# Measured spacings in the planner's prices of TensorE's matmuls and of VectorE's scalings and maxima

## The chip, the cores and the metric

The kernel runs on one core of one Trainium2 chip. The metric is the device time in microseconds of one execution, the median of several; lower is better.

## The reference

Two layers of a hybrid decoder on 528 tokens (16 learned meta tokens and 512 of input) of 1024 channels, in float32. Cut to what matters:

```python
for l in range(DEPTH):                       # DEPTH = 2
    xn = rms_norm(h, norm1_g[l])
    z, xbc, dt_raw, q, k, v, gate_logits = split(xn @ w_in[l])
    y_ssd = ssd_mixer(z, xbc, dt_raw, ...)   # width-4 conv, silu, chunked Mamba-2 scan, gated norm
    y_attn = sliding_window_attention(q, k, v, ...)  # 16 query heads, 4 kv heads, window 128, sinks
    g_ssd, g_attn = split(sigmoid(gate_logits + b_gate[l]))
    merged = g_ssd * (y_ssd @ w_ssd_down[l]) + g_attn * (y_attn @ w_attn_down[l])
    h = h + merged @ w_o[l]
    hn = rms_norm(h, norm2_g[l])
    h = h + square(relu(hn @ w_mlp_up[l])) @ w_mlp_down[l]
return h[:, 16:]
```

## The kernel before

Activations lie transposed: 128 channels on the partitions, 528 tokens along the row. A weight is read in tiles of 1024 input channels by 128 output channels (`wraw`, 512 KB). Products that need near-float32 precision are made of three fp32r products: ScalarE rounds a weight tile to its high half `whi`, POOL or VectorE subtracts to get the low half `wlo` (`weights`, `sub_any`), activations are split in the same way, and `dense` adds hi x hi, hi x lo and lo x hi over the eight blocks of input channels into one PSUM bank. Layer 0 runs its products on two spans of 264 tokens (266 for what the convolution reads); layer 1, whose meta tokens are needed only in part, mostly on one span of 512.

A layer goes through stages. At its start come the norm, v and dt, then k and q with rotary embedding. In the mixer the tiles of xs, B, C, z and the gates are streamed as dense products, and between these matmuls the small work of attention (`attention`) and of the SSD scan (`chunk`, `tail`) is threaded. Then come the two down projections, the output projection, and the MLP in four quarters, dense products almost alone.

Attention works in 36 blocks (five query blocks in layer 0 and four in layer 1, for each of 4 kv heads). A block computes scores in two pairs (`score`); VectorE adds the mask and takes the row maximum in one instruction (`top`, a `tensor_tensor_reduce`, seen in the trace as `CUSTOM_DVE_ANT_0`); ScalarE takes the exponential; VectorE scales four rows by the reciprocal of the sum (`tensor_scalar` on `at`, SBUF to SBUF, with a scalar per row). Then one to three pieces each go through transposes on TensorE, a copy to `ar` on ScalarE, a subtraction into `ar` on VectorE, and the product with v. An SSD chunk (80 of them, 72 of which need an output and 64 a state) has transposes, a state product, and an output of four products on 64 partitions each (`ps<-gm,xdt`).

The order of all of this is not written by hand. While the program is built, a planner (`Flow`) keeps a clock for each engine (`F.t`), adds to it the price of each instruction, and pins every instruction behind the one before it on its engine. A piece of small work is a `Task`, a generator; `dense` calls `tick` after every second matmul, and `tick` lets a task take its next step when its ready time is not later than TensorE's clock:

```python
if (calm or q is not self.queues["attn"]) and t.at(self) <= now:
    self.step(t, q)
```

`now` is `F.t["pe"]`. The ready time is the end of the step's last instruction plus `LATP` = 100 ns where TensorE is next. Where one engine reads what another wrote, `there` adds a hop (`HOP`): 198 ns from TensorE to ScalarE, 235 from VectorE to TensorE, 130 where none is listed. `busy` and `calm` hold steps back while VectorE's or ScalarE's clock is over 3500 ns ahead of TensorE's. `shares` and `turn` delay a VectorE instruction past a POOL instruction where both use the shared port: those of VectorE with two tensor operands in SBUF, or with one operand alone. A scaling by a per-row scalar counts as neither. `tt_any` chooses POOL or VectorE by which clock would end first; for weights VectorE is handed a penalty of 1200 ns. The SP queue's DMAs are pinned in the planner's order as well.

The steps of the change touch `Engine.cost` (the prices of VectorE, ScalarE and POOL) and `mm` (the prices of matmuls). In the trace all VectorE, ScalarE and POOL instructions have line L348, all matmuls L431, and transposes L434.

Of the kernel before, what the change touches and what calls it, by code (L numbers as in the profile page):

```python
# [14 lines left out]
PSUM = bass.MemoryType.PSUM  # L15
# [108 lines left out]
class Flow:  # L124
# [85 lines left out]
    def run(self, e, cost, outs, ins, inst):  # L210
        start = max(self.t[e], self.there(e, outs, ins))
        if self.shares(e, outs, ins):
            start = self.turn(e, start)
            held = self.port[e]
            held.append((start, start + cost))
            del held[:-16]
        self.t[e] = end = start + cost
        self.last = cost
        self.note(e, outs, ins, end)
        self.pin(e, inst)  # L220
# [86 lines left out]
class Engine:  # L307
# [12 lines left out]
    def cost(self, name, n, k, aps):  # L320
        scalars = sum(isinstance(k.get(x), bass.AP) for x in ("scalar", "scale", "bias", "mul"))
        if self._k == "v":
            if name == "reciprocal":
                return 6.4 * n + 60.0
            if name == "tensor_tensor_reduce":
                return n / 0.96 + 165.0
            return n / 0.96 + 62.0 + (58.0 if scalars else 0.0)
        if self._k == "s":
            psum = any(x.space == PSUM for x in aps)
            return n / 1.2 + (48.0 if psum else 86.0) + 93.0 * scalars + (95.0 if "accum_out" in k else 0.0)  # L330
        if k.get("op") == ALU.pow:
            return 190.0 * n + 120.0
        if name == "memset":
            return 40.0
        return n * (2.09 if name == "tensor_tensor" else 3.8) + 125.0
# [19 lines left out]
def hybrid_trunk_kernel(ctx: ExitStack, tc: tile.TileContext, h0, params, consts, rope, wdt, w, out,  # L355
# [69 lines left out]
    def mm(o, lhsT, rhs, start=True, stop=True):  # L425
        n = Engine.size(rhs)
        if rhs.dtype == F32R and n >= 256:
            cost = n / 2.4
        else:
            cost = max(n, 128) * 4 / 2.4 * (0.66 if o.shape[0] == 64 else 1.0)  # L430
        F.run("pe", cost, [o], [lhsT, rhs], PE.matmul(out=o, lhsT=lhsT, rhs=rhs, start=start, stop=stop))  # L431

    def transpose(o, in_, k=P):
# [89 lines left out]
    def dense(spans, tile_, act, evac, after=None, hold=False, by_row=None, late=None, more=(), keep=False):  # L523
# [15 lines left out]
        def product(p, ps, a, b, i):  # L539
            x, k = steps[i]  # L540
            last = p == len(parts) - 1
            if late and last and k >= KD - 2:
                late.pop()()
            whi, wlo = wt[parts[p][0]].slot.parts
            act = parts[p][1]
            mm(ps.t[:, :b - a], (wlo if x == 2 else whi)[:, k, :], (act.lo if x == 1 else act.hi)(k)[:, a:b],
               start=(p == 0 and i == 0), stop=(last and i == len(steps) - 1))
            if i % 2:
                F.tick()
                if held and all(t.done for t in first):  # L550
                    leave()
# [40 lines left out]
    def rms_tok(sq, inv_n, cs, tag, rows=(), bank="ps"):  # L592


        yield {bank: 1, "after": rows, "data": lambda: [x[:, CHUNKS[cs[0]][0]:sum(CHUNKS[cs[-1]])] for x in sq()]}
        ps = Slot("ps")
        for c in cs:
            t0 = CHUNKS[c][0]
            x = sq()
            for i in range(len(x)):  # L600
                mm(ps.t[:, c:c + 1], x[i][:, t0:t0 + P], C("ones"), start=i == 0, stop=i == len(x) - 1)
        yield
        r = sm.tile([P, 5], F32, name=tag, tag=tag)
        x = r[:, cs[0]:cs[-1] + 1]
        V.tensor_scalar(out=x, in0=ps.t[:, cs[0]:cs[-1] + 1], scalar1=inv_n, scalar2=EPS, op0=ALU.mult, op1=ALU.add)
        ps.free()
        G.tensor_tensor(out=x, in0=x, in1=C("mhalf")[:, cs[0]:cs[-1] + 1], op=ALU.pow)
        return r

    def bcast_tok(r, cs_, bank="ps"):  # L610

        for cs in ((0, 1, 2), (3, 4)):
            cs = [c for c in cs if c in cs_]
            if not cs:
                continue
            yield {bank: 1}
            ps = Slot("ps")
            lo, end = CHUNKS[cs[0]][0], sum(CHUNKS[cs[-1]])
            for c in cs:
                t0, n = CHUNKS[c]  # L620
                mm(ps.t[:, t0 - lo:t0 - lo + n], r[:n, c:c + 1].broadcast_to([n, P]), C("ident", n)[:, :n])
            yield ps, ps.t[:, 0:end - lo], lo, end
# [73 lines left out]
    for l in range(depth):  # L696
# [154 lines left out]
        for c in range(5):  # L851
# [4 lines left out]
            x = ps.t[:, 256:256 + NH]  # L856
# [867 lines left out]
```

## Time and profile before

| | us |
|---|---|
| median of 3 runs | 2446.96 (2444.26 to 2449.26) |
| profiled execution, its own time | 2436.77 |
| its span, first to last instruction | 2435.1 |
| busy: TensorE, VectorE, POOL, ScalarE | 2363.5, 1337.1, 1097.8, 1025.4 |

Busy time is the union of an engine's instructions. A matmul's duration in the trace (285 ns for 264 columns) overlaps that of the next one; the spacing from start to start is what it takes of TensorE. A float32 product has two matmul records, an fp32r product one.

### The profile page before, as it was taken

Reading aid. Unit: us, or ns where it says so; the run is one execution under the profiler, and the core shown is the slowest. Engines: PE = TensorE matmul, PEld = TensorE weight load, DVE = VectorE, ACT = ScalarE, POOL = GpSimd, SP = SyncE. Lnnn points to the kernel's source line nnn. Section 1 sums busy time; section 2 is a strip of 40 time slices with the busy share of each in tenths; the row PEclk is TensorE's granted clock in tenths of the full one; section 3 lists DMA queues with packets and bytes.
Section 4 is the critical chain, followed back from the end, with each engine's and each line's share of the span. In section 5 each row is a group of like instructions: output and inputs, shape, how many; then the busy total and the mean of one; then the engine's idle time right before and its main releaser. Section 6 shows DMA issues by size and latency. Waiting matters only on the chain.

```text
span 2435.1 us, 40407 instructions
## 1 busy us (share of the span) xinstructions
PE 2363.5 (97%) x16038; PEld 2143.3 (88%) x16038; DVE 1337.1 (55%) x2509; ACT 1025.4 (42%) x1999; POOL 1097.8 (45%) x651
## 2 busy tenths in 40 slices
PE   6999999999999999999999899999999999999999
PEld 6889899999999999999997788888988788888887
DVE  5787788787522444233246868787875135433221
ACT  4365566564432233222244456556554223333231
POOL 3534434465444334343434454445555543444443
PEclk9999999999999999999999999999999999999999
DMA  4323333343443322222232233324434533222222
GB/s 138 91 75 106 83 102 93 90 116 101 118 177 113 141 79 87 96 87 96 94 136 82 69 100 105 106 73 121 118 93 133 177 121 135 89 95 95 95 95 104
DMA packets 133578, 257.33 MB, mean 106 GB/s; under 512 B 16470, under 2 KB 66318, under 8 KB 133390
## 3 DMA queue, kind: packets, MB, share of 16 engines
q1 hardware_dynamic: 133390, 254.75, 33.4%
q8 instruction: 127, 2.08, 0.3%
q14 instruction: 61, 0.50, 0.1%
HBM read 232.03 MB, written 17.33 MB: 102 GB/s over the span
## 4 chain that ended last, share of the span: by engine, by line
PE 80%; DVE 12%; issue 3%; ACT 2%; POOL 2%; DMA 1%; SPq 0%; DVEq 0%; POOLq 0%; ACTq 0%
PE ps L431 78%; PE ps L434 2%; DVE xb L348 2%; DVE at L348 1%; DVE raw L348 1%; DVE xh L348 1%; DVE rqs L348 1%; DVE scr L348 1%; DVE gm L348 1%; POOL wlo L348 1%; DVE ar L348 1%; DVE mx L348 1%; DMA gm<-ac_dram 0%; DVE qa L348 0%; ACT at L348 0%
## 5 line engine op out<-in xcount | busy, mean ns | idle before, releaser
L348 POOL TENSOR_TENSOR wlo<-wraw,whi 128x1024 fp32r<-128x1024 f32 x328 | 797.5, 2431 | 982.7 <-ACT whi L348 930.4
L348 ACT CAST whi<-wraw 128x1024 fp32r<-128x1024 f32 x340 | 355.5, 1046 | 707.5 <-PE ps L431 421.4
L431 PE MATMUL ps<-hnh,whi 128*128 128x266 f32 (+2 forms) x2048 | 401.2, 312 | 5.3 <-DVE vm L348 4.6
L431 PE MATMUL ps<-hnl,whi 128*128 128x266 f32 (+2 forms) x2048 | 399.3, 311 | 0.0
L431 PE MATMUL ps<-hnh,wlo 128*128 128x266 f32 (+2 forms) x2048 | 391.8, 308 | 0.0
L431 PEld LDWEIGHTS ps<-hnh,whi 128*128 128x128 f32 x2048 | 307.2, 192 | 20.6 <-issue 6.8
L431 PEld LDWEIGHTS ps<-hnl,whi 128*128 128x128 f32 x2048 | 307.7, 192 | 15.1 <-issue 1.3
L431 PEld LDWEIGHTS ps<-hnh,wlo 128*128 128x128 f32 x2048 | 304.0, 190 | 15.2 <-issue 2.3
L348 DVE SCALAR_TENSOR_TENSOR h<-ps,h 128x264 f32<-128x264 f32 (+1 forms) x120 | 62.1, 517 | 308.8 <-PE ps L431 308.8
L348 DVE TENSOR_TENSOR hidl<-s,hidh 128x528 fp32r<-128x528 f32 (+1 forms) x64 | 116.9, 1827 | 88.1 <-ACT s L348 88.1
L431 PE MATMUL ps<-hgl,whi 128*128 128x264 f32 (+1 forms) x768 | 153.7, 322 | 1.3 <-DVE hgl L348 1.3
L431 PE MATMUL ps<-hgh,wlo 128*128 128x264 f32 (+1 forms) x768 | 153.4, 321 | 0.0
L431 PE MATMUL ps<-hgh,whi 128*128 128x264 f32 (+1 forms) x768 | 152.8, 321 | 0.0
L431 PE MATMUL ps<-hidl,whi 128*128 128x264 f32 (+1 forms) x768 | 152.6, 321 | 0.0
L431 PE MATMUL ps<-hidh,whi 128*128 128x264 f32 (+1 forms) x768 | 152.5, 320 | 0.0
L431 PE MATMUL ps<-hidh,wlo 128*128 128x264 f32 (+1 forms) x768 | 152.5, 320 | 0.0
L431 PE MATMUL ps<-y,whi 128*128 128x264 f32 (+1 forms) x768 | 137.0, 320 | 0.0
L431 PEld LDWEIGHTS ps<-hgl,whi 128*128 128x128 f32 x768 | 119.0, 188 | 12.4 <-DVE hgl L348 1.6
L431 PEld LDWEIGHTS ps<-hgh,wlo 128*128 128x128 f32 x768 | 119.5, 189 | 11.0
L431 PEld LDWEIGHTS ps<-hidl,whi 128*128 128x128 f32 x768 | 118.9, 188 | 11.0
L431 PEld LDWEIGHTS ps<-hidh,wlo 128*128 128x128 f32 x768 | 118.8, 188 | 11.0
L431 PEld LDWEIGHTS ps<-hidh,whi 128*128 128x128 f32 x768 | 118.7, 188 | 11.1
(218 smaller groups left out, 3947.5 us busy)
## 6 DMA issues: line engine op xcount, KB each, us to landing
wraw<-w_dram SPq DMA_DIRECT2D x344, 512.0 KB
gm<-ac_dram SPq DMA_DIRECT2D x64, 256.0 KB
et<-ac_dram SPq DMA_DIRECT2D x128, 64.0 KB
t<-au SPq DMA_DIRECT2D x48, 66.0 KB
h<-h_dram SPq DMA_DIRECT2D x8, 264.0 KB
at<-rope_dram SPq DMA_DIRECT2D x4, 528.0 KB
y_dram<-xb SPq DMA_DIRECT2D x4, 528.0 KB
yr<-y_dram SPq DMA_DIRECT2D x8, 264.0 KB
```

The costliest lines, as they stand in the source:

```text
L348: inst = fn(*a, **k)
L431: F.run("pe", cost, [o], [lhsT, rhs], PE.matmul(out=o, lhsT=lhsT, rhs=rhs, start=start, stop=stop))
L434: F.run("pe", 108.0 if in_.shape[1] > 64 else 60.0, [o], [in_], PE.transpose(out=o, in_=in_, identity=C("ident", k)[:, :k]))
```

## The change

Four prices of the planner are replaced. No instruction is added to the program or removed from it; the order in which the planner lays out the instructions, and its choices between POOL and VectorE, follow from the prices.

```diff
             if name == "tensor_tensor_reduce":
-                return n / 0.96 + 165.0
+                return n / 0.96 + 190.0
+            if name == "tensor_scalar" and not any(x.space == PSUM for x in aps):
+                return n / 1.92 + 62.0 + (58.0 if scalars else 0.0)
             return n / 0.96 + 62.0 + (58.0 if scalars else 0.0)
...
         if rhs.dtype == F32R and n >= 256:
-            cost = n / 2.4
+            cost = n / 2.25 + 4.0
         else:
-            cost = max(n, 128) * 4 / 2.4 * (0.66 if o.shape[0] == 64 else 1.0)
+            cost = max(n, 128) * 4 / 2.28 * (0.9 if o.shape[0] == 64 else 1.0)
```

## Rows read from the trace of the kernel before

**Rows 1.** The page's first part: busy us (share of span) and instructions.

```profile
PE 2363.5 (97%) x16038; PEld 2143.3 (88%) x16038; DVE 1337.1 (55%) x2509; ACT 1025.4 (42%) x1999; POOL 1097.8 (45%) x651
```

**Rows 2.** Busy time by stretch: us, engines with instruction counts, clock, DMA share, GB/s.

```profile
0.00:150.00 150.00, 124.81 (x933) 119.99 (x934) 96.37 (x209) 65.65 (x147) 67.76 (x49) 0.98 0.32 104
150.00:650.00 500.00, 486.71 (x3870) 454.72 (x3870) 393.60 (x881) 288.03 (x697) 239.57 (x173) 0.99 0.36 100
650.00:1270.00 620.00, 617.15 (x5051) 615.87 (x5051) 211.54 (x287) 184.17 (x247) 254.65 (x115) 1.00 0.32 112
1270.00:1400.00 130.00, 113.30 (x696) 98.19 (x696) 97.03 (x208) 57.59 (x114) 57.09 (x37) 0.95 0.23 71
1400.00:1850.00 450.00, 441.04 (x2952) 383.19 (x2951) 351.78 (x743) 258.24 (x579) 223.15 (x162) 0.99 0.38 104
1850.00:2435.00 585.00, 580.47 (x2547) 471.34 (x2545) 186.79 (x186) 171.75 (x218) 255.54 (x117) 1.00 0.33 113
```

**Rows 3.** TensorE's waits over the span: us in total, times, longest us.

```profile
PE ps L431 <- DVE acc L348: 13.9, 1, 13.9
PE ps L431 <- DVE mx L348: 6.5, 1, 6.5
...
PE ps L431 <- DVE adt L348: 3.8, 2, 3.1
...
PE ps L434 <- DVE at L348: 2.1, 2, 1.2
```

**Rows 4.** TensorE's waits from 150 to 650 us, first and last kind.

```profile
PE ps L431 <- DVE ar L348: 9.0, 8, 2.3
...
PE ps L431 <- POOL q L348: 0.5, 1, 0.5
```

**Rows 5.** TensorE's waits from 1400 to 1850 us, first and last kind.

```profile
PE ps L431 <- DVE ar L348: 5.5, 5, 1.9
...
PE ps L431 <- DVE zs L348: 0.2, 1, 0.2
```

**Rows 6.** Two dense stretches of 50 us, columns as in rows 2.

```profile
1000.00:1050.00 50.00, 50.00 (x414) 50.00 (x413) 14.66 (x21) 12.73 (x16) 21.36 (x9) 1.00 0.25 85
2150.00:2200.00 50.00, 50.00 (x218) 40.67 (x217) 13.25 (x13) 13.14 (x16) 21.70 (x10) 1.00 0.28 95
```

**Rows 7.** Tile ar: durations in ns min/median/max, first and last start, forms.

```profile
L348 DVE TENSOR_TENSOR ar<-ps,ar x92: 205/680/694, 124.8 to 1664.7; 128x512 fp32r<-128x512 f32 x56, 32x512 fp32r<-32x512 f32 x32, 16x64 fp32r<-16x64 f32 x4
```

**Rows 8.** Groups by form on VectorE: count, busy us, mean ns, idle before.

```profile
L348 DVE TENSOR_SCALAR at<-at,su 128x272 f32<-128x272 f32 x96 | 37.0, 448 | 0.9
...
L348 DVE TENSOR_SCALAR at<-at,su 128x144 f32<-128x144 f32 x32 | 16.9, 591 | 0.3
L348 DVE TENSOR_TENSOR wlo<-wraw,whi 128x1024 fp32r<-128x1024 f32 x12 | 16.1, 1346 | 6.7 <-ACT whi L348 6.7
```

**Rows 9.** Tile at on VectorE, the scalings, columns as in rows 7.

```profile
L348 DVE TENSOR_SCALAR at<-at,su x144: 216/356/2521, 123.4 to 1643.8; 128x272 f32<-128x272 f32 x96, 128x144 f32<-128x144 f32 x32, 16x16 f32<-16x16 f32 x16
```

**Rows 10.** Timeline of layer 0's mixer: start us, us, instruction, idle before.

```profile
244.53 2.37 POOL L348 TENSOR_TENSOR wlo<-wraw,whi 128x1024 fp32r<-128x1024 f32 x1 [5.38 <-ACT whi L348]
...
245.03 1.90 DVE L348 TENSOR_SCALAR mx<-mx 128x4 f32<-128x4 f32 x1
...
247.04 0.68 DVE L348 TENSOR_TENSOR ar<-ps,ar 128x512 fp32r<-128x512 f32 x1
...
247.78 0.49 PE L431 MATMUL ps<-ar,vt 128*128 128x512 f32 x1 [1.93 <-DVE ar L348]
```

**Rows 11.** Timeline of TensorE in a chunk's output, two records to a product.

```profile
301.88 0.66 PE L431 MATMUL ps<-gm,xdt 128*64 128x128 f32 x8 [1.62 <-DVE gm L348]
302.46 0.71 PE L431 MATMUL ps<-xb,st 128*128 128x128 f32 x4
```

**Rows 12.** Timeline of layer 1's start, VectorE and TensorE.

```profile
1339.34 2.40 DVE L348 TENSOR_SCALAR rqs<-rqk 128x32 int32<-128x32 int32 x1
...
1352.67 1.86 PE L431 MATMUL ps<-cst,au 128*128 128x2 f32 x8 [6.46 <-DVE mx L348]
```

## The prediction

> **What bounds the kernel now.** I read the page's first part, then the busy time by stage, then TensorE's waits. TensorE is busy 97% of the span of 2435.1 us [rows 1], so the kernel is a queue of matmuls, and only TensorE's idle time can be won: 2435.1 - 2363.5 = 71.6 us. The stages tell where it lies [rows 2]. Start (0 to 150 us): 25.2 us. Mixer of layer 0 (150 to 650): 13.3. Its down projections, output projection and MLP (650 to 1270): 2.8. Start of layer 1 (1270 to 1400): 16.7. Mixer of layer 1: 9.0. The dense rest: 4.5, mostly after the last matmul. The dense stages are matmul after matmul, and no price in the planner shortens them.
>
> In the starts the largest wait has a fixed place, the sums of squares of the first norm (acc, 13.9); two depend on the order, adt (3.1 the longest) and mx (6.5) [rows 3]. In the mixers the largest wait is for ar, the low half of the transposed probabilities: 9.0 us in 8 waits and 5.5 in 5 [rows 4, 5].
>
> **What the prices do.** The program's order is written by the planner: a step goes into TensorE's order as soon as the planner's TensorE clock passes its ready time. Prices alone change, so no operation is added or removed; the order, and whether a subtraction goes to POOL or VectorE, may change. A dense 264-column matmul goes from 264/2.4 = 110 ns to 264/2.25 + 4 = 121.3, a 512-column one from 213.3 to 231.6. The trace shows 414 in 50 us, 120.8 ns, and 218 in 50 us, 229.4 ns [rows 6]. So the new price is right to 1%, and the old one let the planner's TensorE run 10% ahead of the chip's. That error has a use: between a step's input being made and its use the planner puts as many matmuls as fill the wait by its own count, and on the chip these took 10% longer, which was cover for whatever came late.
>
> **Term 1, the lost cover.** Take one piece of an attention block, from its transposes to its product. The planner's wait is 198 (hop) + 475 (ScalarE copy of 512) + 130 (hop) + 595 (VectorE subtraction) + 100 (LATP) = 1498 ns. At 110 ns that is 13.6 matmuls, on the chip 13.6 x 120.8 = 1643 ns; at 121.3 ns it is 12.35 matmuls, 1492 ns. The cover falls by 0.15 us per such step. By the loops there are some 470 of them: 92 pieces [rows 7] with transposes and product, 72 pairs of scores, and 216 in the SSD chunks. The two mixer stretches show 14 and 11 waits of TensorE (five kinds each, the first and the last of them in [rows 4, 5]), so about one step in twenty is late now. Lower end: only these grow, 25 x 0.15 = 3.8 us. Upper end: a step may be placed 100 ns after its input's end, while the code's own hop from VectorE is 235, so each could wait up to 135 ns, on average 0.068, which over 470 is 32 us. Most steps stand in their queues far longer than that, so I stay near the lower end: the number of late steps doubles, the new ones by half of 0.15 us: 3.8 + 1.9 = 5.7 us. What hides the rest is that one wait of TensorE gives every other pending step the same time back.
>
> **Term 2, the scalings.** Each of the 36 attention blocks scales its four score rows on VectorE right before the transposes. The price of a 272-wide one goes from 403 to 262 ns, of a 144-wide one from 270 to 195; the trace has them at 448 and 591 on average [rows 8]. The median over all sizes is 356, the largest 2521 [rows 9]: the new price is that of an undisturbed one. Planned transposes come 4 x 0.141 = 0.56 us (24 blocks) or 0.30 us (8 blocks) sooner. Ends: 0, if all have that slack, and 24 x 0.56 + 8 x 0.30 = 15.8 us, if none has. TensorE waits for them only twice now, 2.1 us [rows 3]; I take four more waits of 0.5: +2.0 us.
>
> The trace shows what disturbs a VectorE instruction: a 4-wide scaling of mx, issued at 245.03, took 1.90 us and ended as POOL's subtraction (244.53 + 2.37) did; ar, next but one, came late, and TensorE stood 1.93 us [rows 10]. The Trainium skill (SBUF — State Buffer, "SBUF: two separate sides") has the rule: VectorE in a two-port mode and GpSimd hold a shared port pair exclusively for a whole instruction, and the loser blocks. Rows 9 and 10 agree (2521 ns at the longest, against 2.37 us of POOL's subtraction). The planner's function shares doesn't count the scalings by a per-row scalar among those that wait for the port, so a price without it is too low by the rule: POOL is busy 239.57 of 500 us there, and a scaling meets on average 0.48 x 1.2 = 0.58 us more; by that term 2 would be nearer to +4.
>
> **Term 3, the half-height products.** The four products of a chunk on 64 partitions go from 141 to 202 ns each. From their first start to the next matmul's the trace has 302.46 - 301.88 = 0.58 us for four, 145 ns [rows 11]. Here the old price was the right one, and the planner's clock will now run ahead of the chip by 4 x 0.057 = 0.23 us in each of 72 chunks, which is cover lost for what is in flight. Ends 0 and 72 x 0.23 = 16 us; at the one-in-twenty of term 1, 72 x 0.05 x 0.23 = 0.8; I take +1.0.
>
> **Smaller ones.** The maxima cost 25 ns more, two to a step: 0 (ends -1 and 0). Weight splits on VectorE (12 at 1.35 us [rows 8]) may move to POOL, which is idle over half the span [rows 1]: with a slower TensorE clock POOL counts as free more often. That relieves VectorE: -1.0 (ends -2 and 0). The two order-dependent waits of the starts can go or double: 0 (ends -9.6 and +9.6). In the dense stages, where VectorE and ScalarE are under 40% busy, nothing.
>
> **Sum.** 5.7 + 2.0 + 1.0 - 1.0 = +7.7 us. The profiled execution took 2436.8 us (span 2435.1), so 2444.5; the median of the runs, 2447.0, is 10.2 above it, and on that scale I predict 2454.7.
>
> The Trainium skill (TensorE: Matmul & The Clock Gate, "Wait — 56ns, not 53.3ns?") puts a matmul at N/2.4 plus 2.5 ns, 112.5 for 264 columns, by which the old price would be right and the new one 8% too high. Rows 6 do not agree for these fp32r products: 120.8. By that rule of the skill each tight step would be placed 1498 - 12.35 x 112.5 = 0.11 us too soon, and term 1 would at the upper end be 470 x 0.11 = 52 us; same sign, and rows decide.
>
> **Rivals.** *Faster.* A right TensorE clock brings POOL's and VectorE's instructions to where the plan has them, and collisions as in [rows 10] are planned around. What such errors cost now: 13.3 + 9.0 in the mixers and 3.1 + 6.5 in the starts, 31.9 us. The 6.5 is of this kind: a 32-wide VectorE instruction of the query norm took 2.40 us at the head of a chain of them, and TensorE stood 6.46 us for a bank [rows 12]. If half goes and term 1's lower end is still paid: -16 + 4 = -12, so 2435. For it: VectorE's and ScalarE's prices are already close. Against: these collisions last 1 to 2.4 us, and the TensorE error between neighbouring events is 0.15.
>
> *No change.* Steps wait in their queues for longer than the cover lost, late waits shift about, and the sum stays within 0.2% (4.9 us, about what runs of this kernel can tell apart): 2447.
>
> *Much slower.* The first 200 us of layer 0's mixer (attention and SSD at once) idle more than the rest. VectorE is 79% busy over that mixer; if the same side work is packed into 9% fewer matmuls it comes to 86%, and a late VectorE then delays every step behind it in its one queue. From there on each lost 0.15 us is paid by most steps: half of 470 x 0.15 = 35, less what stalls give back, +20: 2467.
>
> **Numbers.** My forecast 0.34, much slower 0.10, faster 0.30, no change 0.26. Faster by over 0.2%: 0.30; within 0.2%: 0.26; slower: 0.44. The forecast's own range is 2450 to 2464 (term 1 from 3.8 to 10, term 2 from 0 to 6). The 8-in-10 range reaches into the faster case and over most of the much slower one: 2432 to 2473.
>
> **What would show it.** Right: TensorE's waits in the two mixers go from 25 to some 50 while their sum rises from 22 us to about 30; more waits for at, ar and gm; dense stretches still 414 and 218 matmuls in 50 us; fewer weight splits on VectorE. Term 2 falls if no wait for at is added; term 1, if the number of waits doesn't grow. The forecast is wrong if the mixers' idle time shrinks, or if a start's waits move by more than the mixers'.

## The result and the profile after

The changed kernel took 2483.6 us (2479.3 to 2488.0, 4 runs) against 2447.1 us before: a ratio of 1.015, interval 1.0126 to 1.0174. It is slower by 36.5 us. The forecast, 2454.7, had the sign and much too small a size, and the time lies outside its range.

The page's first part, as [rows 1]:

```profile
PE 2388.8 (96%) x16038; PEld 2159.0 (87%) x16038; DVE 1343.5 (54%) x2518; ACT 1026.9 (41%) x1999; POOL 1078.1 (43%) x642
```

The profiled execution's span grew from 2435.1 to 2486.2, by 51.1 us. That is more than the 36.5 us between the medians, because the kernel before was profiled in one of its quickest executions (79 of them, run beside the experiments, took 2437.6 to 2453.2 us at mean granted clocks between 0.993 and 0.986) and the changed kernel in the longest of its four. The profiles therefore tell where the time went; the medians tell how much. Two halves are to be seen here. TensorE executes the same 16038 instructions but is busy for 25.3 us more (2363.5 to 2388.8), and it idles for 25.8 us more (71.6 to 97.4). The dense stretches, as [rows 6], have not changed, so the price of a dense matmul was right:

```profile
1000.00:1050.00 50.00, 50.00 (x413) 50.00 (x412) 15.49 (x23) 13.79 (x17) 19.12 (x8) 1.00 0.27 96
2200.00:2250.00 50.00, 50.00 (x218) 40.64 (x217) 13.33 (x14) 14.15 (x18) 21.62 (x9) 1.00 0.27 95
```

To compare stages of equal dense work I cut both traces at the first matmul of each: k and q of layer 0; its mixer; down projections and MLP; start of layer 1; its mixer; the rest. Columns as in [rows 2]: stretch, length, busy us of TensorE and the others, then the granted clock. First before, then after:

```profile
45.70:134.80 89.10, 85.03 (x678) 81.57 (x677) 63.90 (x137) 38.01 (x96) 47.18 (x32) 0.96 0.28 83
134.80:686.40 551.60, 536.96 (x4278) 503.73 (x4277) 416.81 (x938) 308.65 (x741) 264.44 (x188) 0.99 0.35 100
686.40:1255.80 569.40, 566.55 (x4641) 565.85 (x4641) 196.49 (x258) 166.46 (x215) 233.95 (x102) 1.00 0.32 110
1255.80:1372.20 116.40, 100.97 (x601) 87.31 (x601) 77.89 (x154) 47.60 (x95) 50.88 (x35) 0.94 0.28 87
1372.20:1894.40 522.20, 511.97 (x3374) 444.09 (x3373) 392.42 (x832) 287.97 (x631) 257.76 (x185) 0.99 0.37 104
1894.40:2435.10 540.70, 536.07 (x2329) 435.33 (x2327) 170.41 (x157) 157.41 (x194) 232.09 (x99) 1.00 0.32 112
```

```profile
44.20:149.50 105.30, 93.26 (x686) 88.85 (x685) 66.99 (x155) 38.42 (x97) 42.59 (x30) 0.89 0.24 71
149.50:730.80 581.30, 551.07 (x4269) 512.77 (x4268) 426.18 (x927) 308.74 (x739) 253.80 (x182) 0.97 0.33 95
730.80:1300.00 569.20, 566.36 (x4640) 565.65 (x4639) 197.36 (x258) 166.76 (x215) 237.32 (x103) 1.00 0.31 110
1300.00:1416.60 116.60, 105.50 (x621) 91.23 (x619) 74.28 (x159) 48.87 (x97) 49.23 (x35) 0.93 0.27 84
1416.60:1945.50 528.90, 511.87 (x3355) 441.45 (x3355) 389.65 (x829) 287.18 (x629) 251.44 (x182) 0.99 0.36 103
1945.50:2486.20 540.70, 536.23 (x2329) 435.03 (x2327) 169.87 (x157) 157.56 (x194) 232.28 (x99) 1.00 0.32 112
```

Of the 51 us, 16.2 are in k and q of layer 0, 29.7 in its mixer and 6.7 in the mixer of layer 1; the first 45 us are 1.5 shorter, and the dense stages and the start of layer 1 differ by 0.2 us or less. In k and q and in layer 0's mixer the granted clock fell as well, from 0.96 to 0.89 and from 0.99 to 0.97. Here are TensorE's waits in the two mixers (us, times, longest us), in the same cut. First before, where [rows 4, 5] have the waits for ar in a narrower window, layer 0 and then layer 1:

```profile
PE ps L431 <- DVE ar L348: 9.0, 8, 2.3
PE ps L431 <- DVE gm L348: 1.8, 2, 1.6
...
PE ps L431 <- POOL xdd L348: 1.1, 2, 0.9
```

```profile
PE ps L431 <- DVE ar L348: 5.9, 6, 1.9
...
PE ps L431 <- DVE gm L348: 0.6, 2, 0.4
PE ps L431 <- POOL xdd L348: 0.4, 1, 0.4
```

Then after:

```profile
PE ps L433 <- DVE ar L350: 8.5, 7, 2.0
PE ps L433 <- POOL xdd L350: 7.2, 7, 2.1
PE ps L433 <- DVE gm L350: 6.1, 4, 2.2
PE ps L433 <- ACT whi L350: 3.1, 1, 3.1
PE ps L433 <- DVE zs L350: 1.6, 2, 1.4
PE ps L436 <- DVE at L350: 1.5, 1, 1.5
...
```

```profile
PE ps L433 <- DVE ar L350: 9.6, 8, 2.5
PE ps L433 <- ACT gm L350: 3.3, 3, 1.1
PE ps L433 <- POOL xdd L350: 2.5, 3, 1.8
PE ps L433 <- DVE gm L350: 0.8, 2, 0.5
...
```

The waits for ar grew by little, from 14.9 to 18.1 us; most of the growth is in those of the SSD chunks, for xdd and gm, from 3.9 to 19.9 us. Here is the longest wait of the mixer, in order of time (start us, us, instruction, idle before and what ended it):

```profile
563.07 0.37 SPq L230 DMA_DIRECT2D gm<-ac_dram  x1
...
568.60 1.28 ACT L350 ACTIVATE gm<-gm,acs 128x128 f32<-128x128 f32 x4 [5.45 <-DMA gm<-ac_dram]
...
570.57 0.24 ACT L350 COPY btk<-ps 128x128 f32<-128x128 f32 x1
...
570.86 0.42 DVE L350 TENSOR_TENSOR xdt<-ps,dtt 128x256 f32<-128x256 f32 x1
...
571.42 0.61 POOL L350 TENSOR_TENSOR xdd<-xdt,ddt 128x256 f32<-128x256 f32 x1 [5.18 <-DVE xdt L350]
...
572.09 0.30 PEld L433 LDWEIGHTS ps<-xdd,btk 128*128 128x128 f32 x2 [3.29 <-POOL xdd L350]
572.09 0.85 PE L433 MATMUL ps<-xdd,btk 128*128 128x256 f32 x2 [3.08 <-ACT whi L350]
```

Read it from the bottom. TensorE stood 3.08 us for xdd (the row of the weight load says so; the matmul's own row names whi, which ended within 0.01 us of xdd, at 572.04 and 572.03), POOL stood for xdt, and xdt came right after btk on ScalarE; and ScalarE had stood 5.45 us before gm, because gm's load, issued at 563.07, let it start only at 568.60. One late load at the head of ScalarE's order held a whole chunk. Now the clock around that wait, columns as before:

```profile
564.00:568.50 4.50, 4.50 (x41) 4.14 (x40) 1.49 (x3) 0.00 (x0) 2.25 (x3) 1.00 0.81 158
568.50:572.10 3.60, 0.53 (x6) 0.31 (x4) 1.88 (x5) 3.44 (x9) 0.68 (x2) 1.00 0.63 127
572.50:575.90 3.40, 3.40 (x20) 2.74 (x18) 1.60 (x6) 1.41 (x5) 2.95 (x3) 0.50 0.05 9
576.00:580.00 4.00, 4.00 (x32) 3.94 (x33) 3.23 (x9) 0.60 (x2) 2.51 (x4) 1.00 0.61 158
```

TensorE idled, and then ran at 0.50, that is 1.2 instead of 2.4 GHz, for 3.4 us: the wait of 3.1 us cost another 1.7. Not every wait is followed by such a stretch: of the 19 waits of 1 us or more in the two mixers 8 are, within 2.1 us of their end (4 of 10 before). The mean granted clock of the span is 0.992 before and 0.984 after: (1 - 0.992) x 2435 = 19 us and (1 - 0.984) x 2486 = 40 us lost to the clock. So 26 us more of idling and some 21 us more of half clock make up 47 of the 51 us between the profiles. The Trainium skill (TensorE: Matmul & The Clock Gate, "A second HAM failure mode: psum-queue depth-cycling") says that in another kernel frequent short idling between groups of matmuls made the clock swing between its two levels. This trace shows such a swing too, from 1.00 to 0.50 and back around the single wait above.

### The profile page after: what moved, and what is told of

The parts are those of the page before. It is cut to its first block, busy times and chain, and to the rows that moved or that the text cites. A ratio compares the mean times of both kernels' runs of the same rounds, so it can differ in the third digit from the quotient of the medians.

```text
span 2486.2 us, 40389 instructions
## 1 busy us (share of the span) xinstructions
PE 2388.8 (96%) x16038; PEld 2159.0 (87%) x16038; DVE 1343.5 (54%) x2518; ACT 1026.9 (41%) x1999; POOL 1078.1 (43%) x642
## 4 chain that ended last, share of the span: by engine, by line
PE 65%; DVE 5%; ACT 2%; issue 1%; DMA 1%; POOL 1%; POOLq 0%; DVEq 0%; ACTq 0%
PE ps L433 63%; PE ps L436 1%; DVE xb L350 1%; ACT gm L350 1%; DVE at L350 1%; DVE raw L350 1%; DMA gm<-ac_dram 0%; DVE rqs L350 0%; DVE gm L350 0%; ACT at L350 0%; DVE xh L350 0%; ACT whi L350 0%; DVE ar L350 0%; POOL wlo L350 0%; DMA wraw<-w_dram 0%
## 5 line engine op out<-in xcount | busy, mean ns | idle before, releaser
L433 PE MATMUL ps<-hnh,wlo 128*128 128x266 f32 (+2 forms) x2048 | 401.6, 312 | 0.0
L433 PEld LDWEIGHTS ps<-hidl,whi 128*128 128x128 f32 x768 | 118.7, 188 | 11.1
L433 PEld LDWEIGHTS ps<-hidh,whi 128*128 128x128 f32 x768 | 118.7, 188 | 11.1
```

## The experiments

All times are medians, each with runs of the kernel before on the same chip (2445.6 to 2449.4). Idle time is that of TensorE in the two mixers (cut as above; 24.9 us before, 47.3 after) and clock the mean of the span, both of the one profiled execution, which can lie anywhere in its kernel's range: e1's was the quickest of four (2466.5), e7's the longest of ten (2449.8).

| run | fp32r price | other prices | us | ratio to before (95%) | mixers idle us | clock |
|---|---|---|---|---|---|---|
| changed kernel | n/2.25 + 4 | changed | 2483.6 | 1.0126 to 1.0174 | 47.3 | 0.984 |
| e1 | n/2.25 + 4 | before | 2478.3 | 1.0096 to 1.0183 | 41.2 | 0.987 |
| e2 | n/2.4 | float32 changed | 2434.5 | 0.9946 to 0.9975 | 23.2 | 0.993 |
| e3 | n/2.4 | VectorE changed | 2450.2 | 0.9999 to 1.0031 | 24.1 | 0.988 |
| e4 | n/2.25 + 4 | changed, LAT 250 | 2470.0 | 1.0076 to 1.0132 | 37.9 | 0.987 |
| e5 | n/2.25 + 4 | changed, others x 1.1 | 2455.2 | 1.0022 to 1.0049 | 32.1 | 0.990 |
| e6 | n/2.6 | float32 changed | 2419.9 | 0.9884 to 0.9914 | 12.1 | 0.992 |
| e7 | n/2.41 | before | 2443.8 | 0.9979 to 0.9998 | 33.8 | 0.989 |
| e8 | n/2.32 | before | 2452.9 | 1.0023 to 1.0045 | 30.5 | 0.988 |
| e9 | n/2.25 + 4 | changed, late loads | 2461.1 | 1.0035 to 1.0073 | 29.7 | 0.986 |
| e10 | n/2.9 | float32 changed | 2415.7 | 0.9848 to 0.9901 | 6.1 | 0.990 |
| e11 | n/2.6 | float32 changed, late loads | 2442.7 | 0.9967 to 0.9999 | 24.9 | 0.989 |
| e12 | n/2.4 | 0.9 for 64 rows | 2456.3 | 1.0018 to 1.0046 | 31.9 | 0.986 |
| e13 | n/2.24 + 4 | changed | 2491.1 | 1.0160 to 1.0209 | 46.3 | 0.983 |
| e14 | n/2.27 + 4 | changed | 2470.6 | 1.0076 to 1.0116 | 34.1 | 0.985 |
| e15 | n/2.27 + 4 | changed, late loads | 2466.2 | 1.0054 to 1.0095 | 33.0 | 0.985 |
| e16 | n/2.4 | changed | 2440.3 | 0.9961 to 0.9992 | 27.5 | 0.993 |
| e17 | n/2.9 | changed | 2417.3 | 0.9855 to 0.9896 | 11.1 | 0.993 |

A further kernel, e18, had the float32 price of the change and n/3.3 for fp32r (80 ns for 264 columns) and was to show where the gain stops. The order that came of it deadlocks, so it has no time, and the row of prices ends at n/2.9.

**Which price loses.** One part of the change at a time.

```diff
e1: -            cost = n / 2.4
    +            cost = n / 2.25 + 4.0
```

> Only the price of the fp32r matmuls is changed (n/2.25 + 4). Theory A (the lost cover is the whole loss, and each wait also costs clock): most of the 36.5 us returns, 2470 to 2485, TensorE's waits 85 to 95 us, granted clock 0.984 to 0.987. Theory B (the half-height float32 products and the scalings are priced wrongly, and that is the loss): within 10 us of 2447. Theory C (the order of before was a lucky one and any new order loses): anything from 2455 to 2485, not tied to which price.

```diff
e2: -            cost = max(n, 128) * 4 / 2.4 * (0.66 if o.shape[0] == 64 else 1.0)
    +            cost = max(n, 128) * 4 / 2.28 * (0.9 if o.shape[0] == 64 else 1.0)
```

> Only the price of the float32 products is changed (128*4/2.28, and 0.9 instead of 0.66 for 64 rows). Theory A: within 8 us of 2447. Theory B: a good part of the loss, 2457 to 2470, with more waits for gm and xdd in the mixers. Theory C: 2455 to 2485.

```diff
e3: -                return n / 0.96 + 165.0
    +                return n / 0.96 + 190.0
    +            if name == "tensor_scalar" and not any(x.space == PSUM for x in aps):
    +                return n / 1.92 + 62.0 + (58.0 if scalars else 0.0)
```

> Only VectorE's prices are changed (scalings and maxima). Theory A: within 8 us of 2447, at most 2455, with some more waits for at. Theory B: 2455 to 2470. Theory C: 2455 to 2485.

The fp32r price alone loses 32.6 us. VectorE's prices move the time by 4.5 us, their interval touching no change; the float32 price even gains 11.1, which none of the three theories had. Theory B falls, and so does theory C, since the new orders of e2 and e3 do not lose 10 us. The whole change without its fp32r price was drawn later:

```diff
e16 (from after): -            cost = n / 2.25 + 4.0
                  +            cost = n / 2.4
```

> The whole change but for its fp32r price, which stays n/2.4. Theory A: within 10 us of 2447, waits 60 to 75 us. If the other three prices lose together what each alone didn't: 2460 or more.

It came out 8.4 us below the kernel before, so the other three do not lose together either.

**Is it the lead of TensorE's clock in the plan?** Two ways to give cover back while the fp32r price stays.

```diff
e4 (from after): -    LAT = 100.0
                 +    LAT = 250.0
                 -    LATP = 100.0
                 +    LATP = 250.0
```

> The whole change, and the planner's two latencies LAT and LATP raised from 100 to 250 ns, which puts the 0.15 us of cover per step back. Theory A: most of the loss is given back, 2445 to 2460, waits back to 65 to 75 us. Theories B and C: it stays at 2475 or above.

```diff
e5 (from after), in Flow.run and Flow.there:
+        cost *= 1.1 if e != "pe" else 1.0
-                            t = max(t, at + self.HOP.get((e_, e), 130.0))
+                            t = max(t, at + 1.1 * self.HOP.get((e_, e), 130.0))
```

> The whole change, with the planner's prices of VectorE, ScalarE and POOL and all its hops multiplied by 1.1, so that TensorE's clock runs as far ahead of the others in the plan as before (by another route than LAT). Theory A (lost cover, plus the clock that each wait costs): 2440 to 2458, waits of TensorE back to 65 to 75 us, clock 0.990 or more. Theory C (the order of before was a lucky one, any new order loses): 2460 to 2485.

Raising the latencies by the 0.15 us of the prediction won 13.7 us, between what the two sides had expected, and a mere other order at the new price came out the same (e14 below, 2470.6), so e4 decides little. Making VectorE, ScalarE, POOL and the hops 1.1 times as dear, which restores their proportion to TensorE's price and leaves the loads' landing times as they were, won 28.4 of the 36.5. That is 15 us under the quickest of those orders (e14), though TensorE's idling, 79.8 us over the span, stayed above the expected 65 to 75. Of the 37.9 us between the profiles of the changed kernel and e5, 17.2 lie in k and q of layer 0, 21.7 in its mixer and 5.2 in the mixer of layer 1; the start of layer 1 took 4.8 longer.

**Does the time follow the price?**

```diff
e7, e8, e6, e10 (from before):
-            cost = n / 2.4
+            cost = n / 2.41     # e8: n / 2.32; e6, with e2's price: n / 2.6; e10, with e2's price: n / 2.9
```

> Before with the fp32r price n/2.41 instead of n/2.4, a change of 0.4% that makes another order out of the same cover. Theory A: 2441 to 2450. Theory C: 2455 to 2485. The difference to 2445.7 says how much of any other run is the luck of an order.

> Before with the fp32r price n/2.32 (113.8 ns, a third of the way to the new 121.3). Theory A, with the loss in proportion to the cover taken: a third of the 32.6 us of the fp32r price alone, 2452 to 2462. If the loss only sets in once the cover is used up: 2443 to 2450. Theory C: 2455 to 2485, no order in it.

> The float32 price of the change, and the fp32r price moved in the other direction, n/2.6 (101.5 ns for 264 columns against 120.8 measured): more cover than before. Theory A: no slower than the run with the float32 price alone, 2420 to 2436, waits 55 to 65 us. If too much cover costs as well (steps come late, the mixers drag on behind the dense products): 2440 to 2455. Theory C: 2450 to 2485.

> As the run with n/2.6, but n/2.9 (91 ns for 264 columns). Theory A, more cover still pays: 2408 to 2420, waits 45 to 55 us. If cover is enough at n/2.6: 2418 to 2426. If late steps start to pile up at the mixers' ends: 2426 to 2445, with TensorE idle before the attention's down projection.

It does, on both sides of the old price. From the smallest price up: 2415.7 (n/2.9), 2419.9 (n/2.6), 2434.5 to 2456.3 (n/2.4, five orders), 2443.8 (n/2.41), 2452.9 (n/2.32), 2470.6 to 2491.1 (the new price and its neighbours). Prices as close as n/2.4 and n/2.32 can't be told apart within the spread of orders, and from n/2.6 to n/2.9 the gain has all but stopped. So TensorE's clock running ahead in the plan is worth time, and the old price held too little of it. TensorE's waits in the two mixers of e10, in full, beside those of after above:

```profile
PE ps L431 <- DVE xh L348: 2.9, 2, 2.7
PE ps L431 <- DVE ar L348: 1.8, 1, 1.8
```

```profile
PE ps L431 <- DVE gm L348: 1.4, 2, 1.1
```

The waits for xdd are gone and of those for ar one is left. The page's TensorE row of e10 has 2359.4 us busy in 2410.4 of span:

```profile
PE 2359.4 (98%) x16038; PEld 2143.4 (89%) x16038; DVE 1333.3 (55%) x2509; ACT 1023.9 (42%) x1999; POOL 1091.1 (45%) x651
```

**How much is the luck of an order?** e7 hardly changes the cover and gave 2443.8; but e2, e3, e12 and e16, all at n/2.4, lie between 2434.5 and 2456.3, so a new order at the same fp32r price moves the time by about 10 us either way. Nor does one profile's idling in the mixers follow the median closely: e7 has 33.8 us where the kernel before has 24.9.

```diff
e12 (from before): -            ... * (0.66 if o.shape[0] == 64 else 1.0)
                   +            ... * (0.9 if o.shape[0] == 64 else 1.0)
```

> Before with 0.9 in place of 0.66 for the half-height float32 products, nothing else. If the 11 us that the float32 price alone won come from these (TensorE's clock in the plan is moved on at each chunk's output): 2430 to 2440. If from the 5% on all float32 products: 2442 to 2450. As the prediction's term 3 had it: 2446 to 2450.

e12 missed all three expectations: it lost 6.9 us where the float32 price as a whole won 11.1. Which of its two parts e2's gain comes from can't be told at this spread. The change's own order was then drawn twice more, and the small fp32r price once more with all other prices of the change:

```diff
e13, e14 (from after): -            cost = n / 2.25 + 4.0
                       +            cost = n / 2.24 + 4.0     # e14: n / 2.27 + 4.0
e17 (from after):      +            cost = n / 2.9
```

> The whole change with n/2.24 + 4 instead of n/2.25 + 4: another order of practically the same cover. Theory A (cover, with some 10 us of luck): 2465 to 2495. If the new order of the change was an unlucky one and the cover costs little: 2445 to 2462.

> The whole change with n/2.27 + 4: a third order of that cover. Theory A: 2465 to 2493. If the change's order was an unlucky one: 2445 to 2462.

> The three other prices of the change, and n/2.9 for fp32r: a second order at the cover of the run with 2415.7. Theory A: 2405 to 2428. If that run was a lucky order: 2430 to 2445.

Three orders at the new cover: 2470.6, 2483.6, 2491.1; two at n/2.9: 2415.7 and 2417.3. The slowest of the five orders at n/2.4 is 2456.3, so the three levels don't overlap: the loss is the level's, and some 10 us of it may be the order's. (With another price for the loads a kernel at n/2.6 did come out in the middle level: e11, below.)

**What had the cover covered?** In e6, where the trace has the landings, gm's loads take 5.3 us from issue to landing (median of 64); the planner counts 1100 + 262144/360 + 1400 = 3228 ns for its 256 KB. In e9, e11 and e15 these loads land 2000 ns later in the plan.

```diff
e9 (from after; the same in e11 on e6, in e15 on e14), in Flow.dma:
+        late = 2000.0 if "ac_dram" in in_.tensor.name else 0.0
-        self.note("sp", [out], [in_], self.t["dma"] + 1400.0)
+        self.note("sp", [out], [in_], self.t["dma"] + 1400.0 + late)
```

> The whole change, and in the planner the loads from ac_dram (gm and et of the SSD chunks) land 2000 ns later, since the traces show 5.3 us from issue to landing for gm where the planner counts 3.2. Theory A1 (cover was lost, and what it had covered were these loads above all: ScalarE stands before gm, and the chunk's steps behind it): 2455 to 2468, ScalarE's waits for gm's load fall from 40 to under 20 us, TensorE's waits for xdd and gm from 16.7 to under 8. Theory A2 (what it had covered were VectorE's blocks of 1 to 2 us by POOL's port): 2475 to 2490, waits for ar unchanged.

> The run with n/2.6 and the later landing of the loads from ac_dram. Theory A1: little is left to win there, since that run shows 11 us of ScalarE's waits for gm: 2414 to 2422. Theory A2: the same. Should it lose: the chunks start later and the mixers drag on, 2424 to 2435.

> As the run before, with the loads from ac_dram landing 2000 ns later in the planner. If these loads were a part of what the cover had covered: 10 to 25 us below the run before, ScalarE's waits for gm's load under 20 us. If the gain seen at n/2.25 + 4 was its order's: within 10 us of the run before.

ScalarE's waits for gm's loads, after and then e9 (us, times, longest):

```profile
ACT gm L350 <- DMA gm<-ac_dram: 40.4, 23, 5.5
```

```profile
ACT gm L351 <- DMA gm<-ac_dram: 10.6, 9, 2.5
```

The waits went as expected, TensorE's for xdd from 9.8 to 4.5 us with them, and e9 won 22.6 us. But on another order (e15 against e14) the same edit won only 4.4, which by the expectation for e15 makes e9's gain its order's, and with n/2.6 (e11 against e6) it lost 22.8, more than any expectation had. The traces of e14 and e15 show why the waits for loads are not the whole story. ScalarE's for gm's loads fell from 42.0 to 9.9 us, and TensorE's for xdd all but went, but those for ar rose by 9.1 us. TensorE's waits over the span, e14 and then e15:

```profile
PE ps L433 <- DVE ar L350: 13.5, 12, 2.1
PE ps L433 <- POOL xdd L350: 8.0, 10, 2.4
```

```profile
PE ps L434 <- DVE ar L351: 22.6, 22, 2.7
...
PE ps L434 <- POOL xdd L351: 0.2, 1, 0.2
```

And in e5, the best at the new price, ScalarE waited longer for gm's loads than in the changed kernel, 50.6 us. So late loads stand in the chains of the changed kernel, but that they are what the cover had covered is not shown. e11's loss lies in the second quarters of the mixers' dense products (15.5 of the 19.2 us between the mixers of the two profiles), and its cause was not looked for further.

e10 and e17 are faster than both kernels.

## Why the prediction was right in sign and wrong in size

**The bound** held: TensorE is the queue, the dense stages stood still, and the loss lies where side work is threaded in, in k and q of layer 0 and in the mixers.

**Term 1, the lost cover,** is the step that failed, as a size. Its sign is shown by e1, e16, e5 and the row of prices. It said "the number of late steps doubles, the new ones by half of 0.15 us". In the two mixers (cut by work) the number of waits went from 28 to 43, so the count was forecast roughly. But TensorE's idling there went from 24.9 to 47.3 us, 22.4 more where the term had 5.7: 1.5 us to each added wait, twenty times the 0.075 assumed. (Which waits are the added ones can't be told; the mean of all went from 0.87 to 1.08 us.) The cover was worked out on one short chain, a piece of attention, 1.5 us long. The waits came mostly elsewhere, in the chunks: those for xdd, which the prediction did not name, went from 3 to 10 and for gm from 4 to 9, those for ar from 14 to 15. In a chunk a step stands behind a load or behind other work in an in-order queue, as in the chain at 572.09. That ten per cent of such longer chains is what was lost is an argument; no run isolates it. Nor do e4 and e5 show that the cover is a proportion and not a constant: they are one order each and 14.7 us apart, where three orders at the new price are 20.5 apart.

**A term was missing.** No price was put on the clock. The stretches of [rows 2] already had granted clocks of 0.95 to 0.99 beside every stretch with waits and 1.00 beside the dense ones, and the wait of [rows 10] is followed in the same trace by 0.50:

```profile
244.00:247.70 3.70, 1.84 (x15) 1.52 (x13) 3.63 (x9) 1.20 (x4) 2.37 (x1) 1.00 0.00 0
248.20:251.60 3.40, 3.40 (x18) 3.25 (x17) 3.18 (x10) 2.49 (x8) 0.00 (x0) 0.50 0.36 139
251.70:256.00 4.30, 4.30 (x34) 3.91 (x33) 3.76 (x8) 2.44 (x4) 0.95 (x1) 1.00 0.00 0
```

Read with that, the 71.6 us of idle time that the prediction took as all there was to win was too little by the 19 us of half clock. Between the two profiles 21 us of half clock stand beside 26 of idling. By the mean clocks of all executions the half clock took 26 us before (79 of them) and 38 after (4), 12 more, so this case gives 0.5 to 0.8 us of clock for each us of waiting added.

**Term 2** (scalings, +2.0) and the maxima (0) together forecast +2; e3 measured 4.5, interval -0.2 to 7.6. TensorE's waits for at went from two to three over the span of the changed kernel (2.1 to 3.4 us), not up by four. The scalings still run at 494 ns on average and 2581 at the longest, as in [rows 8, 9], so the new price is that of the undisturbed one:

```profile
L350 DVE TENSOR_SCALAR at<-at,su 128x272 f32<-128x272 f32 x96 | 41.5, 494 | 0.9
```

**Term 3** (+1.0) can't be told from the order's luck: its part alone lost 6.9 us, with the other float32 price it won 11.1.

**Smaller ones.** Weight splits on VectorE went from 12 to 10, as forecast. The starts' waits that depend on the order were said to move by up to 9.6 us either way and put at nothing; k and q of layer 0 lost 16.2, half of it clock. This zero failed too, and not by the luck of an order: the stage took 102.5 to 105.6 us in six of the eight kernels at the new price and its neighbours (changed, e1, e9, e13, e14, e15), against 89.1 before, and 92.2 and 88.1 in e4 and e5, which put cover back.

**The rivals.** Faster: refuted; a TensorE clock that is right did not let the plan avoid the collisions, and one that is wrong by 25% (n/2.9 against the measured 120.8 ns) has the fewest waits. No change: refuted. Much slower, +20: nearest in size, but its mechanism isn't what the rows show; VectorE's busy time per mixer hardly moved (416.8 to 426.2 us and 392.4 to 389.7), and most steps still don't wait.

## What to carry to other kernels

In a planner whose clocks drive an in-order queue of the bounding engine, a price that is too low for that engine is a safety margin; making it right takes the margin away, and waits that it had covered come to light. Here a later landing of the loads alone was not shown to account for them, while making the other engines' prices and the hops dearer in proportion won most of the loss back. Price a wait of TensorE with the half clock that may follow it, from the granted clock beside the stretches that have waits. And draw an order twice before a gain or a loss of under 1% is put down to the price that was changed.

## What the runs showed that I had not expected

Some waits of 1 to 3 us are followed by a stretch at a granted clock of 0.50, and in the profiled executions the clock took 19 us of the kernel before and 40 of the kernel after. And five orders at one fp32r price have medians 22 us apart (2434.5 to 2456.3), while the medians of the kernel before, measured beside each group of runs, lie within 4 (2445.6 to 2449.4).
